# A second Strassen pair in each group of the second FFN's up product, and the sums for the down products made in the down stage

## The chip, the cores and the metric

The kernel runs on one core of a Trainium2 chip. TensorE (PE in the profile) multiplies matrices into PSUM, with weight loads (PEld) that overlap the matmuls; VectorE (DVE) and ScalarE (ACT) do elementwise work and evacuate PSUM; GpSimd (POOL) does little here; SyncE (SP) issues the DMAs. The metric is the device time of one execution in microseconds, the median of several runs.

## The reference

Two transformer-like blocks follow each other on one sequence of 256 rows of width 2048, all in float32. The first has differential attention and retention, a cross attention, and a gated FFN of width 5632; the second has a gated spatial mix with a linear recurrent unit, and an FFN of width 6144 with a causal convolution. What the change touches is the two FFNs:

```python
# first block
x = x + (jax.nn.silu(hf @ w_gate[l]) * (hf @ w_up[l])) @ w_down[l]
# second block
up = jnp.einsum('bsd,df->bsf', h, ffn_w_up[l])
up = _causal_dwconv(up, ffn_conv_w[l], ffn_conv_b[l])
gate, val = jnp.split(up, 2, axis=-1)
x = x + jnp.einsum('bsf,fd->bsd', jax.nn.gelu(gate) * val, ffn_w_down[l])
```

`h` is the normalized `x` (256 x 2048), `ffn_w_up` 2048 x 12288, `ffn_w_down` 6144 x 2048.

## The kernel before

**Three matmuls for one product.** Float32 operands are split into a high part and a low remainder: `split` (L179) casts on ScalarE (L181) and subtracts on VectorE (L182). A product of a 128 x 128 block of activations and a 128 x 512 block of weights is then three matmuls of 512 columns (`mm3`, L197: high by high, high by low, low by high). Weights are streamed from HBM in tiles of 128 x 2048, one tile for one *unit*; `push` (L292) splits them piece by piece, 1024 columns as a rule, and `half` (L332) keeps five pieces ahead of the products. The high and the low parts have five buffers each (pools `whi` and `wlo`, L59 and L60).

**Units of kind N and S.** In the FFNs one unit joins a pair of 128-row blocks of the inner dimension with two column blocks of the weights and two halves of the rows, so it is a 2 x 2 by 2 x 2 block product. It is done in one of two ways, given by the strings `KINDS`, `KINDS2` and `KINDS_DOWN` (L25 to L28), read by `kind` (L273): N is the plain way with 8 block products and two weight pieces; S is Strassen's (in Winograd's form) with 7 block products and four pieces a, c, b, d, of which c is 512 wide. An S unit needs sums of weight blocks, made on VectorE in `push` (L317, L322, L323), and sums of activation blocks.

**Activations.** `Quad` (L109) holds a pair of activation blocks, split, with what its kind needs besides: for S four sums (L132 to L135), split in `x`; for D, used by the N units of an up product, one difference (L126). `Pair` (L81) holds the split blocks alone. The up product's eight pairs are made once (`operands`, L587); those of the down product as the up stage goes.

**Stages.** The inner width is done in parts (`PARTS`, `PARTS2`). For each part an up stage runs one *group* for every 512 columns of gate and up: `gemm_q` (L423) over eight units, `quad_group` (L504) with the evacuation (L521 to L528), and then a background generator: `ffn_pairs` (L938) in the first FFN, which transposes the result, and in the second `conv_pairs` (L1217), which transposes gate and value in four sets (L1225), applies the convolution (`conv3`, L1206: L1210 on ScalarE, L1213 on VectorE) and the gelu (L1230, L1231). Such generators move on by one step at each `tick` (L344), that is between the pieces of the next group or, for a part's last group, of the down stage. Then the down stage runs `add_quads` (L567) for two column groups, with `gemm_sum` (L464) over the part's units; its S units, at indices 3 and 5 in the first two parts of each FFN, share product banks, and `add_quads` adds all to `x` in SBUF (L575 to L585). The second FFN has 12 groups in three parts of four; the third part's down product has no S unit.

**PSUM and SBUF.** Eight banks of 512 floats: four in the pool `psg` (tiles "pg"), four in `pss` ("pp"). In `gemm_q` products 2 to 5 take "pg", products 1, 6 and 7 "pp" (L435), held from the first S unit of the group to the last; the transposes take "pp" too. Activations and temporaries are tiles of 128 x 512 floats from one pool of 54 (`tpool`, L61).

**Order.** The order of instructions on each engine is laid out by a scheduler when the program is built (L1376); a piece that isn't ready may be passed by another. One order is written out: `behind` (L316) holds the first weight sum of an S unit behind the evacuation of products 2 and 4 (L524).

Of the kernel before, what the change touches and what calls it, by code (L numbers as in the profile page):

```python
# [12 lines left out]
ALU = mybir.AluOpType  # L13
# [3 lines left out]
P = 128  # L17
S = 256
# [5 lines left out]
PARTS = [(0, 4), (4, 8), (8, 11)]  # L24
KINDS = "NSNSNSNN"  # L25
PARTS2 = [(0, 4), (4, 8), (8, 12)]
KINDS2 = "NNNSNNNN"
KINDS_DOWN = "NNNSNSNN"  # L28
TAIL = 5

# [19 lines left out]
def tile_kernel(ctx, tc, x, xT, mem, memT, par, alibi, rdecay, ident_d, bc_rows, gm_wsT,  # L50
# [3 lines left out]
    V, A, T, G = nc.vector, nc.scalar, nc.tensor, nc.gpsimd  # L54
# [13 lines left out]
    def nm(s):  # L68
        cnt[0] += 1
        return f"{s}_{cnt[0]}"  # L70

    def ft():
        return tpool.tile([P, 2, S], F32, tag="t", name=nm("f"))

    def rt():
        return tpool.tile([P, 2, S], F32R, tag="t", name=nm("r"))

    def flat(f):
        return f.rearrange("p a b -> p (a b)")

    class Pair:  # L81


        def __init__(self, joined):
            self.t = [rt(), rt()]
            self.joined = joined
# [22 lines left out]
    class Quad:  # L109


        def __init__(self, kind, src, gcols=None, psum=True):

            f = ft() if psum else src
            if gcols is not None:
                for k in range(2):
                    A.activation(f[:, k, :], src[:, k, :], AF.Identity, scale=gcols[k])
            elif psum:
                A.copy(f, src)
            self.raw = [rt(), rt()]  # L120
            split(self.raw[0], self.raw[1], f)
            A1, A2 = f[:, :, 0:P], f[:, :, P:]
            e = ft()
            if kind == "D":
                x = rt()
                V.tensor_tensor(e[:, :, 0:P], A1, A2, ALU.subtract)  # L126
                split(x[:, :, 0:P], x[:, :, P:], e[:, :, 0:P])
                self.x = [x[:, :, 0:P], x[:, :, P:]]
            else:

                b = e.rearrange("p a (b n) -> p (a b) n", b=2)
                V.tensor_tensor(b[:, 0, :], A2[:, 0, :], A2[:, 1, :], ALU.add)  # L132
                V.tensor_tensor(b[:, 2, :], A2[:, 0, :], A1[:, 0, :], ALU.subtract)
                V.tensor_tensor(b[:, 1, :], A1[:, 0, :], b[:, 0, :], ALU.subtract)
                V.tensor_tensor(b[:, 3, :], A1[:, 1, :], b[:, 1, :], ALU.add)  # L135
                x = [rt(), rt()]
                split(x[0], x[1], e)
                self.x = [t.rearrange("p a (b n) -> p (a b) n", b=2) for t in x]
# [13 lines left out]
    def gps():  # L152
        return psg.tile([P, 512], F32, tag="g", name=nm("pg"))

    def sps():
        return pss.tile([P, 512], F32, tag="p", name=nm("pp"))
# [22 lines left out]
    def split(hi, lo, src, gcol=None):  # L179
        if gcol is None:  # L180
            A.copy(hi, src)  # L181
            V.tensor_tensor(lo, src, hi.bitcast(F32), ALU.subtract)  # L182
        else:
            A.activation(hi, src, AF.Identity, scale=gcol)
            V.scalar_tensor_tensor(lo, src, gcol, hi.bitcast(F32), ALU.mult, ALU.subtract)

    def xpose_split(src, c, gcols=None, joined=False, quad=None):

        pt = sps().rearrange("p (k s) -> p k s", k=2)
        for k in range(2):  # L190
            for t in range(2):
                T.transpose(pt[:, k, t * P:(t + 1) * P], src[t][:, c + k * P:c + (k + 1) * P], ident)  # L192
        if quad is not None:
            return Quad(quad, pt, gcols)
        return Pair(joined).fill(pt, gcols)

    def mm3(out, lh, rh, start, stop):  # L197

        T.matmul(out, lhsT=lh[0], rhs=rh[0], start=start, stop=False)  # L199
        T.matmul(out, lhsT=lh[0], rhs=rh[1], start=False, stop=False)  # L200
        T.matmul(out, lhsT=lh[1], rhs=rh[0], start=False, stop=stop)  # L201
# [71 lines left out]
    def kind(w, u):  # L273
        if w is w_down or w is w_down2:
            return KINDS_DOWN[u % 8] if u < 2 * (PARTS if w is w_down else PARTS2)[-1][0] else "N"
        return KINDS[u] if w is w_gu else KINDS2[u] if w is w_uv else "N"

# [54 lines left out]
    def half(w, g, u, i, n):  # L332
        while pos[1] < len(pieces) and len(feed) < 1 + LOOKAHEAD:
            push()
        w_, g_, u_, i_, hi, lo = feed.pop(0)
        assert w_ is w and (g_, u_, i_) == (g, u, i)
        if isinstance(hi, list):
            return hi, lo
        return [[t[:, k * n:(k + 1) * n] for k in range(t.shape[-1] // n)] for t in (hi, lo)]
# [4 lines left out]
    def tick():  # L344
        for g in list(bg):
            try:
                next(g)
            except StopIteration:
                bg.remove(g)
# [8 lines left out]
    def need(lst, i):  # L358
        while lst[i] is None:
            assert bg  # L360
            tick()
        return lst[i]
# [101 lines left out]
    def gemm_sum(wap, g, acts, k0, sums_done):  # L464


        M = {}
        n = len(acts)
        ks = [kind(wap, k0 + u) for u in range(n)]
        first, end = ks.index("S") if "S" in ks else n, n - ks[::-1].index("S") if "S" in ks else 0  # L470
        ns, nn = ks.count("S"), ks.count("N")
        total = {11: 2 * nn + ns, 12: 2 * nn + ns, 21: 2 * nn + ns, 22: 2 * nn, 1: ns, 5: ns, 6: ns, 7: ns}
        done = dict.fromkeys(total, 0)

        def prod(m, a, b):
            if m not in M:
                M[m] = gps() if m > 10 else sps()
            done[m] += 1
            mm3(M[m], a, b, done[m] == 1, done[m] == total[m])

        for u in range(n):
            if u == first:
                for v in range(first, end):
                    need(acts, v)
            a = need(acts, u)
            if ks[u] == "N":
                plan = [(0, [(11, a.blk(0, 0), 0), (11, a.blk(1, 0), 1), (21, a.blk(0, 1), 0), (21, a.blk(1, 1), 1)]),
                        (1, [(22, a.blk(1, 1), 0), (22, a.blk(0, 1), 1), (12, a.blk(1, 0), 0), (12, a.blk(0, 0), 1)])]
            else:
                plan = [("a", [(1, a.blk(0, 0), 0), (11, a.blk(1, 0), 1)]),  # L490
                        ("c", [(12, a.sums(3), 0)]),
                        ("b", [(5, a.sums(0), 0), (7, a.sums(2), 1)]),
                        ("d", [(6, a.sums(1), 0), (21, a.blk(1, 1), 1)])]
            for i, ops in plan:
                hi, lo = half(wap, g, k0 + u, i, 512)
                for m, x, b in ops:
                    prod(m, x, (hi[b], lo[b]))
                if u == end - 1 and i in ("a", "d"):
                    sums_done(M, i)
                if not first <= u < end:  # L500
                    tick()
        return M
# [435 lines left out]
    def ffn_pairs(s, acts, i, sums):  # L938
        for p in range(2):
            strassen = sums and KINDS_DOWN[i + p] == "S"  # L940
            acts[i + p] = xpose_split(s, 256 * p, quad="S" if strassen else None)
            yield

    def second_norm(g):
# [7 lines left out]
    for g0, g1 in PARTS:  # L952
        last_part = g1 == PARTS[-1][1]
        acts = [None] * (2 * (g1 - g0))
        for g in range(g0, g1):
            s, finish = quad_group(w_gu, g, hf_a)
# [102 lines left out]
    for g in range(2):  # L1059
# [4 lines left out]
        for t in range(2):  # L1064
            f = flat(ft())
# [3 lines left out]
    for g in range(2):  # L1069
        for o, lst in ((8, gvg), (10, gvb)):  # L1070
            f = flat(ft())
# [114 lines left out]
    for g in range(2):  # L1186
        ps = gemm_tm(w_in2_t, g, h2_a)
        u = []
        for t in range(2):
            f = flat(ft())  # L1190
# [8 lines left out]
    for g in range(4):  # L1199
        add_x(gemm_tm(w_out2, g, y_a), g)  # L1200
        spawn(next_in(g, h3_a, sq3, cols("norm2_g_2", 0, 16), None, KINDS2), 1)

# [14 lines left out]
    def conv_pairs(gate, val, g, acts, i, pause, sums):  # L1217

        for p in range(2):
            y = []  # L1220
            for z, c0 in ((gate, 4 * g + 2 * p), (val, 48 + 4 * g + 2 * p)):
                pt = sps().rearrange("p (k s) -> p k s", k=2)
                for k in range(2):
                    for t in range(2):
                        T.transpose(pt[:, k, t * P:(t + 1) * P], z[t][:, (2 * p + k) * P:(2 * p + k + 1) * P],  # L1225
                                    ident)
                y.append(conv3(pt, c0))
                for _ in range(pause):
                    yield
            A.activation(y[0], y[0], AF.Gelu_apprx_tanh)  # L1230
            V.tensor_tensor(y[0], y[0], y[1], ALU.mult)  # L1231
            if sums and KINDS_DOWN[i + p] == "S":
                acts[i + p] = Quad("S", y[0], psum=False)
            else:
                acts[i + p] = Pair(False).fill(y[0])

    sq_o = Sq(4)
    for g0, g1 in PARTS2:
        acts = [None] * (2 * (g1 - g0))
# [17 lines left out]
    for g in range(4):  # L1257
        f = flat(ft())
# [121 lines left out]
```

## Time and profile before

| what | us |
|---|---|
| median of 3 runs (lowest, highest) | 2568.11 (2567.74, 2568.42) |
| the profiled execution | 2568.99 |
| its span, first to last instruction | 2567.2 |
| mean granted TensorE clock | 0.999 |
| first FFN, up groups of the first part and its down stage | about 770 to 1034 |
| second FFN, up groups of the three parts | about 1767 to 1943, 2031 to 2206, 2294 to 2474 |
| read from HBM | 486.39 MB, 190 GB/s over the span |

Stage times are read from the first and last instructions of the lines named above. All instruction times are of the profiled execution, which took 0.88 us more than the median. An instruction's row has its engine, line, output and inputs by the program's names, shape and count; a time after "<-" is idle time of the engine before it, with what ended it. Successive instructions of one engine overlap, so a stretch's work is counted better by the distance of their starts than by their durations.

### The profile page before, as it was taken

To read this page: it belongs to the slowest core of one execution; us is meant where nothing else is said; L and a number is where in the kernel's file an instruction comes from. 1 tells how busy PE (TensorE), PEld (TensorE's weight loads), DVE (VectorE), ACT (ScalarE), POOL (GpSimd) and SP (SyncE) were. 2 spreads that over 40 slices of the span, in tenths; PEclk is the share of its full clock that TensorE was granted. 3 is DMA by queue.
4 is the path that set the end of the run, shared out by engine and by line. 5 is a ranking of instruction groups with operands and counts; after the bars stand their busy time and mean duration, and the time that the engine had idled before them with its cause. 6 is when DMAs were issued, how large, how long until landed. Compare 5 with 4: busy or idle time off the path is not lost.

```text
span 2567.2 us, 31342 instructions
## 1 busy us (share of the span) xinstructions
PE 2547.2 (99%) x12161; PEld 2135.6 (83%) x12161; DVE 1914.8 (75%) x2448; ACT 1428.6 (56%) x1915; POOL 27.5 (1%) x34
## 2 busy tenths in 40 slices
PE   8999999999999999999999999999999999999998
PEld 7888888888888888888888888888888888888887
DVE  6665565556569888988898667866788878887875
ACT  6555554445455555555555565755565456645653
POOL 0000010000000000000000000000000000000000
PEclk9999999999999999999999999999999999999999
DMA  6455555554445555554555554555554555455563
GB/s 254 170 180 205 194 205 192 188 189 155 153 170 184 198 207 199 196 208 184 213 197 205 205 212 174 181 183 195 181 189 183 206 194 180 182 212 197 180 213 131
DMA packets 72724, 490.51 MB, mean 191 GB/s; under 512 B 8192, under 2 KB 8320, under 8 KB 14592
## 3 DMA queue, kind: packets, MB, share of 16 engines
q1 hardware_dynamic: 72576, 488.52, 52.8%
q8 instruction: 95, 1.56, 0.2%
q14 instruction: 53, 0.43, 0.0%
HBM read 486.39 MB, written 2.10 MB: 190 GB/s over the span
## 4 chain that ended last, share of the span: by engine, by line
PE 97%; DVE 1%; DMA 1%; issue 0%; ACT 0%; POOL 0%; SPq 0%; ACTq 0%; POOLq 0%; DVEq 0%
PE pg L199 24%; PE pg L201 24%; PE pg L200 24%; PE pg L375 10%; PE pg L379 5%; PE pp L201 2%; PE pp L200 2%; PE pp L199 2%; PE pp L192 1%; PE pp L1225 1%; DVE wl L182 0%; DMA w<-in_w_gu_dram 0%; ACT wh L181 0%; DMA w<-in_w_in_f_dram 0%; PE pp L1046 0%
## 5 line engine op out<-in xcount | busy, mean ns | idle before, releaser
L182 DVE TENSOR_TENSOR wl<-w,wh 128x1024 fp32r<-128x1024 f32 x838 | 1021.5, 1223 | 492.1 <-ACT wh L181 488.4
L181 ACT CAST wh<-w 128x1024 fp32r<-128x1024 f32 x838 | 878.9, 1052 | 785.3 <-PE pg L201 593.6
L200 PE MATMUL pg<-wl,r 128*128 128x512 f32 x2687 | 1047.9, 390 | 0.0
L201 PE MATMUL pg<-wh,r 128*128 128x512 f32 x2687 | 1044.0, 390 | 0.0
L199 PE MATMUL pg<-wh,r 128*128 128x512 f32 x2687 | 1034.8, 391 | 0.4 <-DVE f L527 0.4
L201 PEld LDWEIGHTS pg<-wh,r 128*128 128x128 f32 x2687 | 504.5, 188 | 105.1
L199 PEld LDWEIGHTS pg<-wh,r 128*128 128x128 f32 x2687 | 504.5, 188 | 103.6 <-DVE f L527 0.8
L200 PEld LDWEIGHTS pg<-wl,r 128*128 128x128 f32 x2687 | 504.6, 188 | 103.2 <-DVE wl L182 0.6
L375 PE MATMUL pg<-r,wh 128*128 128x512 f32 x1152 | 311.4, 397 | 9.5 <-ACT wh L181 8.1
L375 PEld LDWEIGHTS pg<-r,wh 128*128 128x128 f32 x1152 | 202.2, 190 | 40.8 <-ACT wh L181 8.1
L379 PEld LDWEIGHTS pg<-r,wl 128*128 128x128 f32 x1152 | 169.0, 191 | 18.2
L181 ACT CAST wh<-wt 128x1024 fp32r<-128x1024 f32 x122 | 128.4, 1052 | 97.0 <-PE pg L201 49.0
L182 DVE TENSOR_TENSOR wl<-wt,wh 128x1024 fp32r<-128x1024 f32 x122 | 148.7, 1220 | 43.5 <-ACT wh L181 42.4
L379 PE MATMUL pg<-r,wl 128*128 128x256 f32 x1152 | 177.0, 284 | 0.0
L1213 DVE SCALAR_TENSOR_TENSOR f<-pp,pr,f 128x255 f32<-128x255 f32 x192 | 87.6, 478 | 2.6 <-ACT f L1210 0.6
L201 PE MATMUL pp<-wh,r 128*128 128x512 f32 x211 | 82.2, 390 | 0.0
L317 DVE TENSOR_TENSOR wt<-w 128x1024 f32<-128x1024 f32 x61 | 74.4, 1219 | 10.4 <-DMA w<-in_w_down_dram 6.4
L200 PE MATMUL pp<-wl,r 128*128 128x512 f32 x211 | 82.1, 389 | 0.0
L199 PE MATMUL pp<-wh,r 128*128 128x512 f32 x211 | 82.0, 393 | 0.0
L182 DVE TENSOR_TENSOR r<-f,r 128x512 fp32r<-128x512 f32 (+1 forms) x100 | 64.8, 648 | 4.2 <-ACT r L181 3.4
L181 ACT CAST r<-f 128x512 fp32r<-128x512 f32 (+1 forms) x100 | 59.0, 590 | 15.8 <-DVE f L538 9.4
L1210 ACT ACTIVATE f<-pp,pr 128x256 f32<-128x256 f32 x96 | 53.7, 563 | 24.1 <-DVE f L1213 24.1
(202 smaller groups left out, 1613.1 us busy)
## 6 DMA issues: line engine op xcount, KB each, us to landing
w<-in_w_uv_dram SPq DMA_DIRECT2D x96, 1024.0 KB, 4.8
w<-in_w_gu_dram SPq DMA_DIRECT2D x88, 1024.0 KB, 4.8
w<-in_w_down_dram SPq DMA_DIRECT2D x84, 1024.0 KB, 4.8
w<-in_w_in_t_dram SPq DMA_DIRECT2D x40, 1024.0 KB, 4.8
w<-in_w_in_f_dram SPq DMA_DIRECT2D x39, 1024.0 KB, 4.8
w<-in_w_o_dram SPq DMA_DIRECT2D x16, 1024.0 KB, 4.8
w<-in_w_xk_dram SPq DMA_DIRECT2D x16, 1024.0 KB, 4.7
w<-in_w_xv_dram SPq DMA_DIRECT2D x16, 1024.0 KB, 4.8
```

The lines of the kernel that those rows point to most:

```text
L181: A.copy(hi, src)
L182: V.tensor_tensor(lo, src, hi.bitcast(F32), ALU.subtract)
L192: T.transpose(pt[:, k, t * P:(t + 1) * P], src[t][:, c + k * P:c + (k + 1) * P], ident)
L199: T.matmul(out, lhsT=lh[0], rhs=rh[0], start=start, stop=False)
L200: T.matmul(out, lhsT=lh[0], rhs=rh[1], start=False, stop=False)
L201: T.matmul(out, lhsT=lh[1], rhs=rh[0], start=False, stop=stop)
L317: V.tensor_tensor(sums["b"], b[:, 3:4, :].to_broadcast([P, 2, 512]), b[:, 0:3:2, :], ALU.subtract)
L375: T.matmul(ps[m], lhsT=hi[k][:, m * P:(m + 1) * P], rhs=ops[k].both(k % 2), start=begin and k == 0, stop=stop, skip_group_check=True)
L379: T.matmul(ps[m][:, S:], lhsT=lo[k][:, m * P:(m + 1) * P], rhs=ops[k].hi(k % 2), start=False, stop=False, skip_group_check=True)
L1210: A.activation(y[:, j, :], z[:, j, :], AF.Identity, scale=col("ffn_conv_w_2", 192 + c), bias=col("ffn_conv_b_2", c))
L1213: V.scalar_tensor_tensor(y[:, j, d:], z[:, j, :S - d], col("ffn_conv_w_2", 96 * (2 - d) + c), y[:, j, d:], ALU.mult, ALU.add)
L1225: T.transpose(pt[:, k, t * P:(t + 1) * P], z[t][:, (2 * p + k) * P:(2 * p + k + 1) * P], ident)
```

## The change

In the second FFN's up product, units 2 and 5 of each eight are S, where unit 3 alone was. And for the S units of both down products, the activation sums are no longer made with the rest of the `Quad`: a `Quad` of kind "later" keeps its float source `f`, and `gemm_sum` calls `prepare` for the pair two units ahead. `prepare` holds the same instructions as before: four sums and one split. With no kind "D" or "S" nothing beyond the split of `f` is done at first; for kind "S" `prepare` is called at once.

```diff
-KINDS2 = "NNNSNNNN"
+KINDS2 = "NNSNNSNN"
 KINDS_DOWN = "NNNSNSNN"
...
             split(self.raw[0], self.raw[1], f)
-            A1, A2 = f[:, :, 0:P], f[:, :, P:]
-            e = ft()
+            self.x, self.f = None, f
             if kind == "D":
-                x = rt()
-                V.tensor_tensor(e[:, :, 0:P], A1, A2, ALU.subtract)
+                e, x = ft(), rt()
+                V.tensor_tensor(e[:, :, 0:P], f[:, :, 0:P], f[:, :, P:], ALU.subtract)
                 split(x[:, :, 0:P], x[:, :, P:], e[:, :, 0:P])
                 self.x = [x[:, :, 0:P], x[:, :, P:]]
-            else:
+            elif kind == "S":
+                self.prepare()
+
+        def prepare(self):
+            if self.x is None:
+                f, e = self.f, ft()
+                A1, A2 = f[:, :, 0:P], f[:, :, P:]
 
                 b = e.rearrange("p a (b n) -> p (a b) n", b=2)
                 V.tensor_tensor(b[:, 0, :], A2[:, 0, :], A2[:, 1, :], ALU.add)
...
             if u == first:
                 for v in range(first, end):
                     need(acts, v)
+            if u + 2 < n and ks[u + 2] == "S":
+                need(acts, u + 2).prepare()
             a = need(acts, u)
...
-            acts[i + p] = xpose_split(s, 256 * p, quad="S" if strassen else None)
+            acts[i + p] = xpose_split(s, 256 * p, quad="later" if strassen else None)
...
             if sums and KINDS_DOWN[i + p] == "S":
-                acts[i + p] = Quad("S", y[0], psum=False)
+                acts[i + p] = Quad("later", y[0], psum=False)
```

## The prediction, made before the result was known

> **What bounds the kernel now.** I read the page's busy table first, then the chain that ended last.
>
> ```profile
> PE 2547.2 (99%) x12161; PEld 2135.6 (83%) x12161; DVE 1914.8 (75%) x2448; ACT 1428.6 (56%) x1915; POOL 27.5 (1%) x34
> PE 97%; DVE 1%; DMA 1%; issue 0%; ACT 0%; POOL 0%; SPq 0%; ACTq 0%; POOLq 0%; DVEq 0%
> ```
>
> TensorE is busy for all but 20 of 2567 us and holds 97% of the chain. Matmuls overlap, so busy time alone doesn't show that it runs at its pace; the starts in the timeline do.
>
> ```profile
> 1876.42 0.39 PE L201 MATMUL pg<-wh,r 128*128 128x512 f32 x1
> 1876.65 0.39 PE L199 MATMUL pg<-wh,r 128*128 128x512 f32 x1
> 1876.87 0.39 PE L200 MATMUL pg<-wl,r 128*128 128x512 f32 x1
> 1877.10 0.39 PE L201 MATMUL pg<-wh,r 128*128 128x512 f32 x1
> ```
>
> A 512-column matmul lasts 0.39 us, but the next starts 0.227 us later (0.68 for three). The second FFN's up groups keep this pace, by windows from one evacuation (L521) to the next; then the waits of 1763 to 2475 us, the whole second FFN but its last piece:
>
> ```profile
> 1805.88:1850.64 44.76, 44.76 (x206) 37.03 (x206) 36.31 (x50) 27.17 (x35) 0.00 (x0) 1.00 0.53 187
> 2377.57:2422.33 44.76, 44.76 (x206) 37.04 (x206) 36.32 (x49) 27.16 (x35) 0.00 (x0) 1.00 0.52 187
> PEld pg L200 <- DVE wl L182: 0.6, 2, 0.3
> ACT wh L181 <- PE pg L201: 215.9, 163, 3.2
> DVE wl L182 <- ACT wh L181: 128.4, 123, 2.1
> ```
>
> The columns of a window are its length, then busy time of PE, weight loads, DVE, ACT, POOL. A group is 7 N units of 24 matmuls, an S unit of 21 and 16 short transposes: 189 x 0.227 = 42.9 us, and the other 1.9 is the transposes. So nothing is idle. Over 700 us TensorE waited 0.6 us for split weights; the other way about, the split (ACT cast, then DVE subtract) waited for buffers that TensorE still held. The bound is the number of matmuls, with DVE the next engine, at 36.31 of 44.76 us (81%).
>
> [...]
>
> **The matmuls removed.** An N unit makes 8 products of 3 matmuls (L442 to L447), an S unit 7. Each of 12 up groups turns one N unit into S: 12 x 3 = 36 matmuls x 0.227 = **8.17 us** off TensorE, 0.68 a group. DMA bytes, transposes and the down products' matmuls stay as they are.
>
> **The DVE work added in the up groups.** What one S unit needs beyond an N unit, by rows of the groups:
>
> ```profile
> L182 DVE TENSOR_TENSOR wl<-w,wh 128x1024 fp32r<-128x1024 f32 x838 | 1021.5, 1223 | 492.1 <-ACT wh L181 488.4
> L317 DVE TENSOR_TENSOR wt<-w 128x1024 f32<-128x1024 f32 x61 | 74.4, 1219 | 10.4 <-DMA w<-in_w_down_dram 6.4 <-DMA w<-in_w_gu_dram 3.9
> L322 DVE TENSOR_TENSOR wt<-wt,w 128x512 f32<-128x512 f32 x61 | 41.7, 684 | 0.1
> L182 DVE TENSOR_TENSOR r<-w,r 128x512 fp32r<-128x512 f32 x71 | 48.2, 684 | 1.7 <-ACT r L181 1.7
> 1942.93 1.22 DVE L317 TENSOR_TENSOR wt<-w 128x1024 f32<-128x1024 f32 x1
> 1944.07 0.69 DVE L526 TENSOR_TENSOR f<-pg,f 128x512 f32<-128x512 f32 x1
> 1944.67 0.68 DVE L527 TENSOR_TENSOR f<-pg,f 128x512 f32<-128x512 f32 x1
> ```
>
> S splits three 1024-wide pieces and a 512-wide one, N two 1024-wide; S adds L317 (1024) and L322 and L323 (512 each). That is two 1024-wide and three 512-wide operations more. Back to back they start 1.14 and 0.60 us apart, so 2 x 1.14 + 3 x 0.60 = **4.1 us** a group (by their durations 4.5). ACT gets one 1024- and one 512-wide cast more, some 1.6 us on 27. DVE goes to 36.3 + 4.1 = 40.4 of 44.76 - 0.68 = 44.08 us: 92%. Two windows show what TensorE does at such a load:
>
> ```profile
> 1073.07:1115.47 42.40, 42.40 (x193) 35.18 (x192) 38.04 (x43) 24.07 (x27) 0.00 (x0) 1.00 0.56 200
> 1957.00:1990.00 33.00, 33.00 (x146) 27.11 (x145) 31.62 (x44) 20.08 (x26) 0.00 (x0) 1.00 0.49 185
> 1865.39 1.23 DVE L182 TENSOR_TENSOR wl<-wt,wh 128x1024 fp32r<-128x1024 f32 x1 [2.14 <-ACT wh L181]
> ```
>
> The first FFN's up group has three S units, DVE at 90%, and loses nothing; nor does the second's down stage at 96% for 33 us. The third row is DVE in mid-group with nothing to do, its casts waiting for a buffer: the lead of the splits is full there. Where in a group the work falls matters too. The S unit at index 3 has its sums made while the last group's evacuations and convolutions also run; now they come one unit earlier, the second set for unit 5 about when the convolutions end, with two N units behind it to catch up. The peak is hardly higher, the valley filled. I take **0** here (cover: 4.4 - 0.7 = 3.7 us of idle DVE left a group; bounds 0 and, in the rivals, all of the gain).
>
> One more of the eight activation pairs for the up product is prepared as S, not D: four 128-wide sums and a 512-wide split instead of three 256-wide operations, half a microsecond of DVE, once, while TensorE works on the output projection, long before its use: 0 (0.5 without that cover).
>
> **The sums moved.** One set, before:
>
> ```profile
> 1850.64:1895.44 44.80, 44.80 (x206) 37.06 (x206) 37.77 (x55) 27.69 (x36) 0.00 (x0) 1.00 0.53 189
> 1885.46 0.68 DVE L182 TENSOR_TENSOR r<-f,r 128x512 fp32r<-128x512 f32 x1
> 1886.06 0.28 DVE L132 TENSOR_TENSOR f<-f 128x128 f32<-128x128 f32 x1
> 1886.27 0.28 DVE L133 TENSOR_TENSOR f<-f 128x128 f32<-128x128 f32 x1
> ```
>
> Splits of activations like the first one start 0.60 before the next instruction, the sums 0.20 apart: four sums and a split are 1.4 us of DVE, which is the 37.77 against 36.31, and 0.6 of ACT. Eight sets (two in each of two parts of both FFNs) leave the up groups, where without the move these groups would stand at 41.9 of 44.1, and go to the first half of the down stage, in units 1 and 3 of its first column group. Nothing is issued to a DMA queue; the new reader keeps one float tile a pair alive longer, from a pool of 54. The stage that receives them:
>
> ```profile
> 1940.20:1984.00 43.80, 43.80 (x202) 36.33 (x201) 39.59 (x56) 28.25 (x37) 0.00 (x0) 1.00 0.46 172
> 951.42:991.00 39.58, 39.58 (x180) 32.87 (x179) 33.76 (x40) 20.32 (x22) 0.00 (x0) 1.00 0.54 192
> 1954.91 1.23 DVE L182 TENSOR_TENSOR wl<-wt,wh 128x1024 fp32r<-128x1024 f32 x1 [2.14 <-ACT wh L181]
> 1988.67 0.68 DVE L585 TENSOR_TENSOR xt<-xt,pg 128x512 f32<-128x512 f32 x1
> 1989.37 0.40 PE L199 MATMUL pg<-wh,r 128*128 128x512 f32 x1
> ```
>
> In the first FFN 33.8 + 2.8 = 36.6 of 39.6: nothing, as nothing is won in its up groups, which lose no time now. In the second, 39.6 + 2.8 = 42.4 of 43.8, 97%, because the last group's convolutions run there too. The first set fits the hole of 2.14 us before 1954.91, as its input is long there. The second comes where DVE is full (1957 to 1990: 1.4 us idle in all), and pushes what is queued on DVE behind it, up to L585, which frees a bank: it ends at 1989.35 and a product starts at 1989.37, with nothing to spare. A set costs between 0 and 1.4 us there; I take 0.5 for the second set and 0 for the first, so **+1.0 us** for two parts (bounds 0 and 4 x 1.4 = 5.6).
>
> **Sum.** The profiled execution took 2568.99 us, 2567.2 of it span. 2568.99 - 8.17 + 1.0 = 2561.8. It was 0.88 above the median of the runs, 2568.11; on the median, 2560.9. I predict **2561.0 us**.
>
> **The rivals.**
>
> *The moved sums lengthen the down stages.* For it: 97%, and the bank freed in the last moment. Against: TensorE can take other pieces first, as it did with the d piece below. All four sets on the path: 2568.1 - 8.2 + 5.6 = 2565.5.
>
> *DVE becomes the bound in the up groups.* If DVE can be no busier than the 90 to 92% planned (first FFN: 38.04 of 42.40, 89.7%), a group takes 40.4 / 0.897 = 45.0 us, 0.9 over the 44.08, and 12 x 0.9 = 11 us eat the gain: 2571. At 91% it is 44.4 and 2564. Against: both windows above run without loss, so they aren't limits. The middle: 2566.
>
> *Slower: TensorE waits for a bank at the fourth set of transposes.* Products 1, 6 and 7 take banks of the pool "pp" (4), as each transposed convolution input does. Before they were held in one unit; now from unit 2 to unit 5, which leaves one bank.
>
> ```profile
> 1868.21 0.60 PE L1225 MATMUL pp<-ident,f 128*128 128x128 f32 x4
> 1873.46 0.60 PE L1225 MATMUL pp<-ident,f 128*128 128x128 f32 x4
> 1877.89 2.29 DVE L1213 SCALAR_TENSOR_TENSOR f<-pp,pr,f 128x254 f32<-128x254 f32 x5
> 1879.37 0.39 PE L199 MATMUL pp<-wh,r 128*128 128x512 f32 x1
> ```
>
> The third set of transposes, at 1868.21, has its bank read until about 1878.4, 10.1 us later; the fourth came 5.3 us after it. If TensorE stood still for the difference, 4.8 us a group, that is 12 x 4.8 = 58 us: 2618. It decides from 0.68 us a group, where the gain is gone. Against: product 6 (1879.37) already waited for that bank, and TensorE did another unit's products meanwhile without a gap; the order on each engine is laid out at build time round such waits. [...]
>
> *The 36 matmuls fewer don't shorten TensorE's path.* If its load were the 2135.6 us of weight loads, something else would set the pace of the starts, and fewer matmuls would only widen their gaps: 2568.1. Against: the starts stay 0.227 apart whatever DVE and ACT do beside them. [...]
>
> **How the numbers follow.** Forecast, within 1.5 us of 2561: 0.62. Moved sums 0.14, DVE bound 0.14, bank 0.06, no effect 0.04. About 0.2% (5.1 us) is what a measurement of this kernel can tell from none, so faster means below 2563.0. Of the moved sums 0.05 lies below it, of the DVE bound 0.03: faster 0.70, same 0.09 + 0.11 + 0.04 = 0.24, slower 0.06. The range goes from 2559.3 (no cost of the moved sums, and a spread of 0.6) to 2566.5, which takes in the first rival and half of the second: 0.83.
>
> **What would show it.** Right: up groups of 44.08 us with 203 rows of PE, and no PE wait above a microsecond in all; DVE at 40.4 a group; the down stage's first half 44 us still. The first rival shows as PE waiting for L585 or L182 at the end of that half, the second as PE waiting for L182 in every group, the third as a gap before L1225 that ends with L1213. The prediction is wrong if the scheduler lays the second S unit's splits later than the products need them, which no row of before can tell.

## The result: 2597.3 us, 1.1% slower, and the profile after

The changed kernel takes 2597.26 us (median of 4 runs, 2596.40 to 2598.31) where the kernel before, run beside it, takes 2568.27 (2567.74 to 2568.77). The ratio is 1.0113, 95% interval 1.0096 to 1.0131: slower, by 29 us, where 7 us less was forecast. From the page of the profiled execution (span 2594.6 us), the busy table and the chain that ended last:

```profile
PE 2553.1 (98%) x12125; PEld 2135.6 (82%) x12125; DVE 1966.1 (76%) x2511; ACT 1448.5 (56%) x1939; POOL 27.6 (1%) x34
PE 95%; DVE 3%; issue 1%; DMA 1%; ACT 1%; POOL 0%; SPq 0%; ACTq 0%; POOLq 0%; DVEq 0%
```

The 36 matmuls are gone (12161 before, 12125 now), but TensorE is busy 6 us longer, and DVE, 1% of the chain before, has 3%. Fewer matmuls that keep TensorE busy for longer must have become slower in places, so two things have to be found: idle time, and slow matmuls. TensorE's waits in the second FFN (1763 to 2500 us; engine, output and line, what it waited for, us in all, times, longest):

```profile
PE pg L204 <- DVE f L528: 15.5, 6, 4.7
PE pg L205 <- DVE wl L187: 4.2, 2, 2.1
PE pg L204 <- DVE xt L592: 3.0, 3, 1.5
```

Before, this view was empty; the weight loads' own view had one line, of 0.6 us. Now TensorE waits for the first operation of an up group's evacuation (L528, before L521: it frees a bank), and in the down stages for split weights (L187) and for L592 (before L585). The timeline of TensorE at the longest of these, the end of the third up group of the first part, has start, duration, operation and, in brackets, the idle time before it:

```profile
1895.02 0.39 PE L206 MATMUL pg<-wh,r 128*128 128x512 f32 x1
1900.12 0.79 PE L204 MATMUL pg<-wh,r 128*128 128x512 f32 x1 [4.71 <-DVE f L528]
1900.71 0.63 PE L205 MATMUL pg<-wl,r 128*128 128x512 f32 x1
1901.14 0.63 PE L206 MATMUL pg<-wh,r 128*128 128x512 f32 x1
```

The start at 1900.12 comes 5.10 us after the one before, 4.87 more than the usual 0.227. The matmuls behind it start 0.43 us apart instead of 0.227. Windows of 5 us round the stop show the reason in the granted clock (the number ahead of the last two):

```profile
1890.00:1895.00 5.00, 5.00 (x23) 4.13 (x23) 4.26 (x8) 2.43 (x3) 0.00 (x0) 1.00 0.80 280
1895.00:1900.00 5.00, 0.41 (x2) 0.00 (x0) 4.79 (x7) 2.09 (x4) 0.00 (x0) 0.93 0.82 306
1900.00:1905.00 5.00, 4.88 (x12) 3.82 (x13) 4.88 (x8) 2.68 (x4) 0.00 (x0) 0.50 0.11 46
1905.00:1910.00 5.00, 5.00 (x23) 4.10 (x22) 0.56 (x1) 1.64 (x3) 0.00 (x0) 0.89 0.01 2
```

In the 5 us window behind the stop the clock is half, 0.50: 12 matmuls, where the window before the stop has 23.

**A measure for all runs.** Take each distance between two successive matmul starts, less the median distance for that shape (0.227 us for 512 columns), and add it up over 1763 to 2500 us: these *late starts* count stops and slow stretches alike. They are 2.4 us before and 39.7 after. 39.7 - 2.4 less the 8.2 of the matmuls saved is 29.1, the 29.0 that the kernel lost; for all runs below, the same sum comes within 1.5 us of the measured difference. The loss is therefore all there, in three places: a stop of 4.87 us at the end of the third up group of each of the three parts with 1.4 to 3.0 us lost at half clock (0.50, starts 0.43 us apart) behind it; 0.6 to 0.8 at the ends of second groups; and about 7 us in each of the two down stages.

### The profile page after: what moved, and what is told of

Its sections match the earlier page's. It is cut to its first block, busy times and chain, and to the rows that moved or that the text cites. A ratio compares the mean times of both kernels' runs of the same rounds, so it can differ in the third digit from the quotient of the medians.

```text
span 2594.6 us, 31350 instructions
## 1 busy us (share of the span) xinstructions
PE 2553.1 (98%) x12125; PEld 2135.6 (82%) x12125; DVE 1966.1 (76%) x2511; ACT 1448.5 (56%) x1939; POOL 27.6 (1%) x34
## 4 chain that ended last, share of the span: by engine, by line
PE 95%; DVE 3%; issue 1%; DMA 1%; ACT 1%; POOL 0%; SPq 0%; ACTq 0%; POOLq 0%; DVEq 0%
PE pg L204 23%; PE pg L206 23%; PE pg L205 23%; PE pg L380 10%; PE pg L384 5%; PE pp L206 3%; PE pp L205 3%; PE pp L204 3%; DVE wl L187 1%; PE pp L197 1%; PE pp L1232 1%; ACT wh L186 0%; DMA w<-in_w_uv_dram 0%; DMA w<-in_w_in_f_dram 0%; DVE r L187 0%
## 5 line engine op out<-in xcount | busy, mean ns | idle before, releaser
L187 DVE TENSOR_TENSOR wl<-w,wh 128x1024 fp32r<-128x1024 f32 x826 | 1006.2, 1223 | 448.1 <-ACT wh L186 443.5
L205 PE MATMUL pg<-wl,r 128*128 128x512 f32 x2627 | 1028.5, 392 | 4.2 <-DVE wl L187 4.2
L204 PE MATMUL pg<-wh,r 128*128 128x512 f32 x2627 | 1010.7, 394 | 18.5 <-DVE f L528 15.5
L206 PE MATMUL pg<-wh,r 128*128 128x512 f32 x2627 | 1025.4, 391 | 0.0
L204 PEld LDWEIGHTS pg<-wh,r 128*128 128x128 f32 x2627 | 495.9, 189 | 124.5 <-DVE f L528 15.4
L206 PEld LDWEIGHTS pg<-wh,r 128*128 128x128 f32 x2627 | 495.9, 189 | 103.4
L186 ACT CAST wh<-wt 128x1024 fp32r<-128x1024 f32 x146 | 153.8, 1054 | 152.1 <-PE pg L206 102.4
L187 DVE TENSOR_TENSOR wl<-wt,wh 128x1024 fp32r<-128x1024 f32 x146 | 178.4, 1222 | 50.6 <-ACT wh L186 48.3
L322 DVE TENSOR_TENSOR wt<-w 128x1024 f32<-128x1024 f32 x73 | 89.1, 1220 | 16.1 <-DMA w<-in_w_uv_dram 7.5
L205 PE MATMUL pp<-wl,r 128*128 128x512 f32 x247 | 96.2, 390 | 0.0
L204 PE MATMUL pp<-wh,r 128*128 128x512 f32 x247 | 95.8, 393 | 0.0
L206 PE MATMUL pp<-wh,r 128*128 128x512 f32 x247 | 94.9, 391 | 0.0
L186 ACT CAST r<-w 128x512 fp32r<-128x512 f32 x83 | 50.9, 617 | 38.4 <-DMA w<-in_w_gu_dram 24.2
L187 DVE TENSOR_TENSOR r<-f,r 128x512 fp32r<-128x512 f32 (+1 forms) x100 | 65.2, 652 | 6.7 <-ACT r L186 6.0
```

The source lines that it names most:

```text
L322: V.tensor_tensor(sums["b"], b[:, 3:4, :].to_broadcast([P, 2, 512]), b[:, 0:3:2, :], ALU.subtract)
```

## The experiments

Three theories stood at first. A: the banks that products 1, 6 and 7 hold from unit 2 to unit 5 make the fourth transposes late, and with them the evacuation. B: VectorE's added work makes the stops. C: the down stages lose time to the moved sums, apart from the up groups. The results of all twelve kernels, each against the kernel before in its own comparison:

| run | us, median (lowest to highest) | ratio, 95% interval | late starts in the second FFN |
|---|---|---|---|
| kinds_only | 2589.87 (2589.43 to 2591.34) | 1.0084, 1.0069 to 1.0099 | 32.8 |
| later_only | 2578.10 (2576.51 to 2579.05) | 1.0036, 1.0023 to 1.0049 | 12.4 |
| s45 | 2572.36 (2570.73 to 2575.09) | 1.0014, 1.0005 to 1.0024 | 14.6 |
| no_wsum | 2569.97 (2568.48 to 2571.25) | 1.0005, 0.9996 to 1.0014 | 12.4 |
| s45_old | 2572.72 (2571.66 to 2574.34) | 1.0013, 1.0004 to 1.0021 | 14.0 |
| held_banks | 2576.95 (2573.84 to 2578.37) | 1.0027, 1.0015 to 1.0039 | 9.4 |
| both_u1 | 2572.29 (2571.20 to 2574.82) | 1.0013, 1.0004 to 1.0022 | 5.7 |
| down_no_wsum | 2574.54 (2573.07 to 2575.08) | 1.0018, 1.0008 to 1.0027 | 6.8 |
| one_tick | 2568.09 (2564.92 to 2569.63) | 0.9993, 0.9984 to 1.0002 | 9.6 |
| s45_mix | 2563.50 (2562.20 to 2564.26) | 0.9975, 0.9965 to 0.9985 | 5.5 |
| s45_u1 | 2561.16 (2560.49 to 2562.08) | 0.9967, 0.9954 to 0.9979 | 3.9 |
| one_tick_u1 | 2560.67 (2559.68 to 2562.89) | 0.9967, 0.9955 to 0.9979 | 2.5 |

The kernel before took 2568.8 us beside the first four, 2569.41 beside the next four, 2569.36 beside the next three and 2569.42 beside the last.

### The two parts of the change alone

kinds_only is the kernel before with

```diff
-KINDS2 = "NNNSNNNN"
+KINDS2 = "NNSNNSNN"
```

> The two S units of the up groups alone; the sums for the down products stay where they were. Theory A (banks and tile order): products 1, 6 and 7 keep three of the four banks of the pool pp from unit 2 to unit 5, the fourth set of transposes comes late, and what is first written behind its convolution in the source (the c piece of unit 5, the copy of product 1 for the evacuation) is laid out late, so the stops of 4.9 us at group ends stay: some 23 us lost in the up groups. Theory B (DVE is the bound): the sums are back in the third and fourth groups, DVE at 41.9 of 44.1, so more is lost there than now: 2600 or more. Theory C (the moved sums are to blame): the 14 us lost in the down stages are gone and the up groups lose nothing: 2561. With A for the up groups and C for the down stages: 2583.

later_only is the changed kernel with that line set back, so that only the sums are moved.

> The sums made in the down stage alone, one S unit in eight as before. Theory A: no bank is held longer, nothing is late: 2568 within 3 us. Theory B: the same or a little less, as DVE has less to do in the up groups and they were not bound: 2566 to 2569. Theory C: the down stages lose what they lose in the changed kernel, some 13 to 14 us: 2582.

They cost 21.1 us (2589.87 - 2568.8) and 9.3 us (2578.1 - 2568.8); together 30.4, and the whole change 29.0. The expected times were missed, the first (A with C, 2583) by 7 us and the second (C, 2582) by 4. But each part loses time in its own place, the kinds in the up groups and the moved sums in the down stages, as C has it. TensorE's waits in the second FFN, of kinds_only first and then of later_only:

```profile
PE pg L199 <- DVE f L521: 22.0, 8, 7.0
```

```profile
PE pg L205 <- DVE wl L187: 4.1, 4, 1.9
PE pg L204 <- DVE xt L592: 0.4, 1, 0.4
```

With the kinds alone the stops at the third groups are longer in the first two parts, 7.2 us. ScalarE's timeline of kinds_only has the copy of product 1 (L512) behind a cast that waits for the last of the down product's sums (L135):

```profile
1899.13 0.62 ACT L181 CAST r<-f 128x512 fp32r<-128x512 f32 x1 [2.50 <-DVE f L135]
1899.65 0.58 ACT L512 COPY f<-pp 128x512 f32<-128x512 f32 x1
```

With the sums moved these stops are 4.9 us. So the second half of the change does help the first, and costs more elsewhere than it gives. The two halves aren't independent, then, and the totals add up because two differences cancel: late starts in the up groups are some 30 us with the kinds alone and 23 in the changed kernel, those in the down stages 10 with the moved sums alone and 14 in the changed kernel.

### The up groups: bank or load?

s45 is the changed kernel with the two S units next to each other, behind the transposes, so that the banks are held shortly:

```diff
-KINDS2 = "NNSNNSNN"
+KINDS2 = "NNNNSSNN"
```

> The changed kernel with its two S units at 4 and 5 in place of 2 and 5: the same matmuls, the same work on DVE, the same sums in the down stage. Theory A: all four sets of transposes are issued before the first S unit takes banks, so the stops at group ends go: 24 us less than the changed kernel, 2573 (2561 if the down stages' loss goes with it). Theory B: 12.7 us of DVE work for the two units now fall on 9.6 us of TensorE, so no better than the changed kernel: 2597 or more. Theory C: the down stages' 14 us stay, the up groups change little.

no_wsum is the changed kernel without the sums of weights of the up product (L322, L327, L328): pieces b and d are split from the raw weights, so it computes something else. VectorE has some 5 us less in a group.

```diff
-            if i == "a":
+            if i == "a" and w is not w_uv:
...
-            if i == "c":
+            if i == "c" and w is not w_uv:
...
-                src = sums.pop(i).rearrange("p b n -> p (b n)")
+                src = (raw[:, 1024:2048] if w is w_uv else
+                       sums.pop(i).rearrange("p b n -> p (b n)"))
```

> The changed kernel without the weight sums of the second up product: pieces b and d split raw weight columns in place of sums (left out: L322, L327 and L328 for this product, 24 sets of 2.3 us of DVE, 56 us in all; the output is not the reference's). DVE falls below its load before the change, from 40.4 to 35.7 us a group. Theory B: the up groups' stops go, 2597 - 23 = 2574 or less. Theory A: the banks are held as long and the fourth transposes still come late, so the stops of the up groups stay to at least a half: 2586 or more.

Both took the stops of the up groups away. s45 does so with all of VectorE's work and against B, no_wsum with the banks held as long as ever and against A. In no_wsum the fourth set of transposes in the third group still leaves 17 us after the third:

```profile
1866.04 0.60 PE L1233 MATMUL pp<-ident,f 128*128 128x128 f32 x4
1883.08 0.60 PE L1233 MATMUL pp<-ident,f 128*128 128x128 f32 x4
```

The copy of product 1 comes at 1891.2 there, 5 us before the changed kernel's, and TensorE doesn't wait. So neither theory is enough alone: with the S units at 2 and 5, the stops need the late transposes and the added work together, and go when either is taken away. What both act on shows in three views of the changed kernel at the stop of 1900. TensorE, third and fourth set of transposes (L1232) and the last matmul of products 1, 6 and 7:

```profile
1865.27 0.60 PE L1232 MATMUL pp<-ident,f 128*128 128x128 f32 x4
1882.74 0.39 PE L206 MATMUL pp<-wh,r 128*128 128x512 f32 x1
1886.38 0.60 PE L1232 MATMUL pp<-ident,f 128*128 128x128 f32 x4
```

ScalarE:

```profile
1886.64 2.00 ACT L186 CAST wh<-w 128x1024 fp32r<-128x1024 f32 x2 [2.96 <-DMA w<-in_w_uv_dram]
1888.54 0.56 ACT L1217 ACTIVATE f<-pp,pr 128x256 f32<-128x256 f32 x1
1889.00 0.61 ACT L186 CAST r<-w 128x512 fp32r<-128x512 f32 x1
1895.05 0.61 ACT L186 CAST r<-f 128x512 fp32r<-128x512 f32 x1
1896.51 0.57 ACT L519 COPY f<-pp 128x512 f32<-128x512 f32 x1
```

VectorE:

```profile
1898.06 0.69 DVE L521 TENSOR_TENSOR f<-pp,f 128x512 f32<-128x512 f32 x1
1899.38 0.68 DVE L528 TENSOR_TENSOR f<-pg,f 128x512 f32<-128x512 f32 x1
```

The third set leaves at 1865, the fourth at 1886, 21 us later (5.3 before), because three of four "pp" banks are held. Its convolution follows on ScalarE at 1888.54; at once behind it comes the c piece of unit 5 (1889.00), then other casts, and then the copy of product 1 (L519, 1896.51). That product was finished by 1883.13 at the latest, so the copy was 13.4 us late, though ScalarE had been idle for 2.96 us in that time. L521 and L522 need the copy, L528 follows them, and TensorE waits for L528. The order of the program as it was built gives a reason why the copy stands behind work it doesn't need: in it, tiles of one pool are handed out in the order in which the source writes them first (without exception among 278 "pp" and 262 "pg" tiles, and almost so in the pool of 54), and the copy's tile, the c piece and the convolution's output are all tiles of that pool. That is read off the order, not shown by a run; giving the copy a tile of its own was not tried.

held_banks asks for the bank alone. It is the kernel before with its one S unit at unit 2 and its early evacuation put off to unit 5, with no second unit's load:

```diff
-KINDS2 = "NNNSNNNN"
+KINDS2 = "NNSNNNNN"
...
+                    if wap is w_uv and u == 5:
+                        sums_done(M, "ad"[i])
...
-                    if "S" not in ks[u + 1:] and i in "ad":
+                    if wap is not w_uv and "S" not in ks[u + 1:] and i in "ad":
```

> The kernel before with its single S unit of the second FFN's up groups at unit 2 instead of 3, and the copy and sums that free the banks of products 1, 6 and 7 put off to unit 5, where the changed kernel has them: the three banks are held as long as in the changed kernel, with no second unit's sums (VectorE at 36.3 us a group, not 40.4). Nothing is saved, so 2568 us is no loss. If banks held from unit 2 to unit 5 are enough by themselves for the stop at the third groups' ends: 2580 to 2590 us, with three stops of over 4 us. If late transposes and a full VectorE are both needed (as the runs with one or the other taken away suggest): 2567 to 2571 us, with the fourth transposes still late in their group but no stop over 1 us.

2576.95 us: neither expectation. The fourth transposes of the third group are as late as in the changed kernel (first row: TensorE, timeline) and there is no stop there. But at the end of the fourth group, where the sums for down unit 5 come too, there are two stops, one a part (second row: waits):

```profile
1885.90 0.60 PE L1227 MATMUL pp<-ident,f 128*128 128x128 f32 x4
```

```profile
PE pg L199 <- DVE f L523: 4.7, 2, 2.4
```

```profile
1942.51 0.28 DVE L135 TENSOR_TENSOR f<-f,f 128x128 f32<-128x128 f32 x1
1944.09 1.23 DVE L182 TENSOR_TENSOR wl<-w,wh 128x1024 fp32r<-128x1024 f32 x1 [1.30 <-ACT wh L181]
1947.16 0.68 DVE L523 TENSOR_TENSOR f<-pg,f 128x512 f32<-128x512 f32 x1
```

VectorE, in the last rows, was idle for 1.30 us just before the evacuation (L523) that TensorE waited for, and in the fourth group's window it is busy for 84%:

```profile
1896.00:1941.00 45.00, 45.00 (x208) 37.13 (x207) 37.88 (x52) 27.86 (x37) 0.00 (x0) 1.00 0.54 189
```

So VectorE need not be busier than 84% for a stop. But late transposes with a set of sums behind them don't always make one: the third group has both, in the same order, and its evacuation still comes in time. Its fourth set of transposes leaves 16 us behind the third, that of the fourth group 18.

one_tick takes the late bank away and leaves both the kinds and the load. In the changed kernel the transposes of the first three groups of a part are two pieces apart; here they are one apart, as those of the last group, made in the down stage, already are, so that all four sets have their bank before unit 2 takes three:

```diff
-            spawn(conv_pairs(gate, val, g, acts, 2 * (g - g0), 1 if g == g1 - 1 else 2, g1 < PARTS2[-1][1]))
+            spawn(conv_pairs(gate, val, g, acts, 2 * (g - g0), 1, g1 < PARTS2[-1][1]))
```

> The changed kernel with one edit: in every up group of the second FFN the four sets of transposes are one product piece apart (before: two, one only in the last group of a part), so that all four have their bank before unit 2 takes three. VectorE's work is the same. If the late bank of the fourth set is what pushes back the c piece, the copy of product 1 and the evacuation of the group behind it: the stops of 4.9 us at the third groups' ends go with the half-clock stretches behind them, and only the loss in the down stages is left, 2574 to 2578 us. If VectorE's load alone makes the stops: 2590 us or more. If the four sets so close together make a new jam at the group's start, late starts show within the first 10 us of a group.

All stops in the up groups are gone: 2568.09 us, 29 less than the changed kernel, and 6 below the expected range, as the down stages lost less too. The third group in its window (fourth number: DVE), then the copy and L528 of that group from the timeline by line (x1, duration in ns as minimum, median and maximum, start):

```profile
1851.00:1895.00 44.00, 44.00 (x204) 36.46 (x203) 39.86 (x54) 28.61 (x38) 0.00 (x0) 1.00 0.49 180
```

```profile
L519 ACT COPY f<-pp x1: 576/576/576, 1885.2 to 1885.2; 128x512 f32<-128x512 f32 x1
L528 DVE TENSOR_TENSOR f<-pg,f x1: 682/682/682, 1891.3 to 1891.3; 128x512 f32<-128x512 f32 x1
```

The copy is 11 us earlier, L528 8 us, and TensorE is not idle in this window with VectorE at 39.86 of 44 us, 91%. This is the run that decides: with the banks free in time, VectorE's load costs nothing. The convolutions come earlier with their transposes, so the run shows what early transposes are worth, and not which of the steps behind them on ScalarE and VectorE matters most.

### The down stages

In later_only, VectorE's timeline at the border from the first column group to the second:

```profile
1975.93 0.69 DVE L187 TENSOR_TENSOR r<-f,r 128x512 fp32r<-128x512 f32 x1
1976.53 0.28 DVE L137 TENSOR_TENSOR f<-f 128x128 f32<-128x128 f32 x1
1979.76 0.68 DVE L187 TENSOR_TENSOR r<-f,r 128x512 fp32r<-128x512 f32 x1
1984.01 1.23 DVE L187 TENSOR_TENSOR wl<-w,wh 128x1024 fp32r<-128x1024 f32 x1 [1.53 <-ACT wh L186]
1985.15 0.68 DVE L582 TENSOR_TENSOR f<-pp,f 128x512 f32<-128x512 f32 x1
```

and TensorE's:

```profile
1990.66 0.39 PE L204 MATMUL pg<-wh,r 128*128 128x512 f32 x1
1992.91 0.50 PE L205 MATMUL pg<-wl,r 128*128 128x512 f32 x1 [1.86 <-DVE wl L187]
1993.54 0.63 PE L204 MATMUL pg<-wh,r 128*128 128x512 f32 x1
```

The second set of sums runs from 1976.5 to its split at 1979.8, and the first sum of the evacuation (L582) comes at 1985.15. Before, the same operation came six microseconds earlier:

```profile
1979.05 0.68 DVE L575 TENSOR_TENSOR f<-pp,f 128x512 f32<-128x512 f32 x1
```

The 1.4 us of the set don't make six, and VectorE sat idle for 1.53 us in between: again what counts is what is ordered behind what. The evacuation then falls on the splits of the next weights, and TensorE stops for one of them. Two runs on later_only tell place from load. both_u1 makes both sets before unit 1:

```diff
-            if u + 2 < n and ks[u + 2] == "S":
-                need(acts, u + 2).prepare()
+            if u == 1:
+                for v in range(n):
+                    if ks[v] == "S":
+                        need(acts, v).prepare()
```

> The kernel with only the moved sums (KINDS2 NNNSNNNN, 2578.1 us), with the second set of sums for a down group made together with the first, before unit 1, instead of before unit 3. VectorE has the same work in the down stage. If the second set does its harm by its place (its tile and its four additions lie in front of the pieces and the evacuation of the first group), the starts that are 2.0 us late near 1990 and 2259 us, and the slow ones behind them, go and it is 2569 to 2572 us. If the harm is that VectorE has these additions in the down stage at all, it stays at 2577 to 2580 us. If two sets at one place delay unit 1's or 3's weights, there are new late starts before 1985 us and it is above 2580 us.

down_no_wsum leaves the sums of weights of the second FFN's down products out, with the same edit as in no_wsum but for `w_down2`; it too computes something else.

> The kernel with only the moved sums (2578.1 us), with the sums of weights left out for the S units of the second FFN's down products (the pieces b and d are split from the raw weights instead, so the output is not the reference's): 2.6 us of VectorE for each S unit, 5.2 us for a group of the down stage. If VectorE's load in the down stage decides, the late starts near 1990 and 2259 us go and it is 2567 to 2570 us. If the order of the work decides whatever the load is, it stays at 2575 to 2578 us.

both_u1 has VectorE do the same work in the same stage and is 2.9 us above the kernel before in its comparison, where later_only is 9.3 above; in it the first sum of the evacuation is back at 1981.80:

```profile
1981.80 0.68 DVE L584 TENSOR_TENSOR f<-pp,f 128x512 f32<-128x512 f32 x1
```

The stops near 1990 and 2259 are gone; what is left are starts 0.6 to 0.8 us late near 1970 and 1973. down_no_wsum, with 10 us less of VectorE in a down stage, is 5.1 us above and still stops for 1.42 us at 1989. The place of the second set is worth at least as much as a relief of 10 us of load (the intervals of the two ratios overlap). The expectation that load alone would do it (2567 to 2570) fell; the time is half a microsecond below what was expected if the order alone decides (2575 to 2578), so the load has a part in it.

### Together

s45_old is the kernel before with the S units at 4 and 5: the saving with no moved sums.

> The kernel before with one edit: KINDS2 is NNNNSSNN, so the second FFN's up groups have their two S units side by side at 4 and 5; the sums of activations stay where they were before. 36 matmuls fewer than before (8.2 us at 0.227). If the loss of the change is made of two separate parts (stops of TensorE at the ends of third groups, which the place of the two S units decides, and moved sums, which cost some 9 us by themselves): 2560 to 2562 us, with no start of TensorE in the second FFN more than 1 us late. If two S units in an up group cost something wherever they stand (the VectorE work added, 4.1 us a group): 2566 us or more. If the down stages lose time for another reason than the moved sums, the late starts of 1.7 to 3.7 us at the first group's end in the down stages stay and it is 2570 us or more.

2572.72, a miss by 11 us, and a place of loss that the expectation didn't have. (The time falls in the ranges of the two other branches, but the down stages have no such late starts, and s45_u1 below shows that two S units don't cost wherever they stand.) Almost nothing is lost in the third groups or the down stages, but at the end of the fourth group of the first two parts TensorE stops for 3.89 us (waits, then VectorE):

```profile
PE pg L199 <- DVE f L521: 7.5, 2, 3.7
```

```profile
1934.85 0.68 DVE L182 TENSOR_TENSOR r<-f,r 128x512 fp32r<-128x512 f32 x1
1935.45 0.28 DVE L132 TENSOR_TENSOR f<-f 128x128 f32<-128x128 f32 x1
1939.88 0.68 DVE L182 TENSOR_TENSOR r<-f,r 128x512 fp32r<-128x512 f32 x1
1941.62 0.68 DVE L514 TENSOR_TENSOR f<-pp,f 128x512 f32<-128x512 f32 x1
```

The sums for down unit 5 (L132 on, with their split at 1939.88) stand right ahead of the early evacuation (L514). It isn't VectorE's load alone: the third group has a set of sums too and no stop, and in one_tick VectorE is busy for 41.69 of 45 us in the fourth group (here for 41.01) without one. With the S units at 4 and 5 it pays to move that set, and it is the place in the down stage that was bad; whether another order could keep it in the fourth group was not tried.

s45_mix moves the set of unit 5 alone, to before unit 1, and s45_u1 both; both stand on s45 with the edit of both_u1, and s45_mix has besides

```diff
-                acts[i + p] = Quad("later", y[0], psum=False)
+                acts[i + p] = Quad("S" if i + p == 3 else "later", y[0], psum=False)
```

> The changed kernel with its second FFN's S units at 4 and 5 (no stop at the third groups' ends), the sums for down unit 3 made where the kernel before makes them, with its transposes in the third group, and those for unit 5 made before unit 1 of the down group. The third group has room for its set, the fourth has not (3.89 us late at 1941 and 2206 us with both sets in the old place), and one set before unit 1 was free of late starts over 0.5 us. 36 matmuls fewer, 8.2 us: 2560 to 2563 us. If sums for the down stage cost wherever they are made: 2566 us or more.

> The changed kernel with its second FFN's S units at 4 and 5 and both sets of sums for a down group before unit 1. Two sets before unit 1 left four late starts of 0.6 to 0.8 us, 3.3 us in all with what stands around them, where no other edit was made; 36 matmuls fewer take 8.2 us: 2563 to 2566 us, 2 to 3 us more than with one set of the two left in the up stage. If the up groups and the down stages hang together otherwise (S units at 4 and 5 leave VectorE with a backlog at the end of the fourth group that runs into the down stage): 2568 us or more.

Both are faster than the kernel before. The order between them was expected the wrong way round: with one set left in the third group, 2563.50, 2.3 us more than with none (2561.16). s45_u1 saves 8.2 us of 2569.36, what 36 matmuls at 0.227 are worth; the interval of its ratio spans 5.4 to 11.8 us, so the close match is in part luck. one_tick_u1 joins the two cures on the changed kernel's own S units, 2 and 5 (one_tick with the edit of both_u1):

> The changed kernel, its S units at 2 and 5, with both cures: transposes one piece apart (it took away the stops in the up groups) and both sets of down sums before unit 1. If the loss of the change is these two places and nothing else: 2561 to 2563 us, the 8.2 us of the 36 matmuls earned in full, as with the S units at 4 and 5. If S units at 2 and 5 have a price of their own, in the up groups or in VectorE's backlog at the border to the down stage: 2565 us or more.

2560.67 us, 8.75 below the kernel before, and the view of TensorE's waits in the second FFN is empty. With the transposes one piece apart, the units' places have no price that shows. It cannot be told from s45_u1 (ratio 0.9967 for both); either is the version to keep. In s45_u1 the windows of the second and third up group and of the fourth show what VectorE bears:

```profile
1807.00:1851.00 44.00, 44.00 (x204) 36.40 (x203) 39.99 (x54) 28.49 (x37) 0.00 (x0) 1.00 0.54 191
1851.00:1895.00 44.00, 44.00 (x203) 36.43 (x202) 39.98 (x55) 28.44 (x37) 0.00 (x0) 1.00 0.53 192
1895.00:1940.00 45.00, 45.00 (x207) 37.23 (x207) 40.89 (x56) 28.95 (x39) 0.00 (x0) 1.00 0.52 187
```

## Why the prediction was wrong

- **The bound and the saving: right.** Where nothing stops TensorE, 36 matmuls fewer are worth 8.2 to 8.75 us (s45_u1, one_tick_u1; each interval reaches some 3 us either way) against the 8.17 worked out. With it falls the rival that the matmuls don't leave the path.
- **"I take 0 here", the up groups: the step that failed.** As a sum of VectorE's time it was right: at 40 of 44 us TensorE loses nothing (one_tick, s45_u1), and the rival of a limit at 90% is wrong. But it priced load as a sum over a group, and the term was set by what is ordered behind what: some 23 us of late starts in the changed kernel, and some 30 with the kinds alone. It takes both the late transposes and the added work: with 5 us less of VectorE's work a group the stops went as well (no_wsum). The prediction named what would make it wrong, splits laid out later than the products need them; what was late was the evacuation, by the c piece and the copy of product 1.
- **The bank rival: one of the two causes, wrong place and price.** The three banks held from unit 2 to unit 5 did put the fourth transposes off, by 16 us more than before. TensorE did not stand still for them, as the argument against the rival had it, since it took other products. That argument looked at the waiting transposes only and not at what stands behind them on ScalarE and VectorE: the convolution, and behind it the copy that the group's evacuation starts with. The gap ended 14 us later, before L204 and not before L1232, in three groups of twelve, and cost some 23 us, not 58. Its 0.06 was too small: I ruled out the place that I had looked at and took that for the mechanism.
- **"+1.0 us" for the moved sums: mis-sized, and beyond its bounds (0 to 5.6).** It measured 9.3 by itself (later_only), and the down stages of the changed kernel have some 14 us of late starts. That the second set pushes on VectorE's queue was right; that it can cost no more than its own 1.4 us was the error. It moved the evacuation by 6 us, and TensorE's stop of 2.0 us was followed by starts 0.43 us apart, which cost 1.7 to 2.3 us more and which no term of the sum had.
- **The move's use was missed.** It was noted that without the move the up groups would stand at 41.9 of 44.1 us, and this was given no price. With two S units and the set of unit 5 left in the fourth group, s45_old stops for 3.89 us there; s45_u1, with the sums moved to a good place, doesn't.

Open is why the changed kernel stops for 4.87 us at third groups and for 0.6 to 0.8 at second ones. The fourth set of transposes comes late in the second, the third and the fourth group alike (20, 21 and 16.5 us behind the third set of its group), and the end of the fourth group has no stop at all; what tells the groups apart wasn't varied here. Open too is whether the copy's place behind the c piece is what carries the delay, as no run gave the copy a tile of its own.

## What to carry to other kernels

When a change lets an accumulator hold its bank longer, follow the other users of that pool to what is queued behind *them*, up to the next evacuation: here TensorE took other work past the waiting one, and paid 14 us later and elsewhere. Price moved work by what is ordered behind it and not by its own length; a busy share of 91% on VectorE cost nothing here in one order, and 84% in another came with 7 us of late starts. And give a short piece of work that must be moved two places to be tried, since one place cost 9 us and another 3 for the same instructions.

## What the runs showed of the hardware that was not expected

A stop can cost more than its length. Behind the three stops of 4.87 us in the changed kernel (1900, 2176 and 2452 us) and one of 2.3 us (2271) the granted clock is 0.50 for some 3 to 7 us, and 512-column starts are 0.43 us apart. It isn't strictly a matter of the stop's length. In one_tick, a start that came 1.98 us late at 1990.2 was followed by

```profile
1991.00:1995.00 4.00, 4.00 (x12) 3.10 (x11) 3.31 (x5) 0.66 (x1) 0.00 (x0) 0.57 0.25 107
```

and of two stops of 3.89 us in s45_old the first, at 1941, kept the full clock and the second, at 2206, lost it (the first column group of numbers after the window is PE, the clock stands third from the end):

```profile
1945.00:1950.00 5.00, 4.62 (x20) 3.86 (x21) 4.97 (x8) 2.67 (x4) 0.00 (x0) 1.00 0.18 74
```

```profile
2210.00:2215.00 5.00, 4.44 (x11) 3.50 (x12) 4.97 (x8) 2.67 (x4) 0.00 (x0) 0.50 0.19 79
```

What made the clock fall behind one of the two equal stops and not behind the other was not shown by any run.
